# Key norms by float32r products on channels, and a block inversion moved to GpSimd, in a hybrid RWKV-7 / FoX block

## The chip, the cores and the metric

The kernel runs on one core of a Trainium2 chip. The metric is the device time of one execution in microseconds, the median of several runs. The core's engines work from queues of their own: TensorE (products and transposes; PE in the profile, its weight loads PEld), VectorE (DVE), ScalarE (ACT), GpSimd (POOL) and SyncE (SP), which issues most of the DMAs. An instruction waits on semaphores for what it reads and for the buffers that it overwrites, and whatever is behind it in the same queue waits too.

## The reference, cut to what matters

One decoder layer for 256 tokens behind 16 meta tokens (272 rows), width 2048, all in float32. It is an input projection, RWKV-7 time mixing and FoX forgetting attention side by side (16 heads of 64 each), gates, and a SwiGLU network:

```python
def _rms(x, g):
    xf = x * lax.rsqrt(jnp.mean(x * x, axis=-1, keepdims=True) + RMS_EPS)
    return xf * g

def _rwkv7(z, ...):                       # z: r, k, v and three low-rank parts
    ...
    kk = heads(k * k_k)
    kk = kk / jnp.maximum(jnp.sqrt(jnp.sum(kk * kk, axis=-1, keepdims=True)), 1e-12)
    ...
    y = _wkv7_scan(rh, dh, kh, vh, -kk, kk * ah)
    ...                                   # group norm, bonus, gate

def _fox(z, q_g, k_g, f_bias):
    ...
    q = _rms(q.reshape(B, L, FOX_HEADS, HEAD_DIM), q_g)
    k = _rms(k.reshape(B, L, FOX_HEADS, HEAD_DIM), k_g)
    ...                                   # causal softmax with forgetting, times v

def _layer(h, ...):
    proj = _rms(h, n1) @ w_in
    y_a, y_b = _rwkv7(...), _fox(...)
    merged = g_a * (y_a @ w_a) + g_b * (y_b @ w_b)
    h = h + merged @ w_o
    gate, up = jnp.split(_rms(h, n2) @ w_gu, 2, axis=-1)
    return h + (silu(gate) * up) @ w_dn
```

Two places matter here. The keys of both branches are normalised head by head, over 64 channels. And the scan over time is computed in chunks of 64 tokens, for which a unit triangular matrix of each chunk and head has to be inverted.

## The kernel before, in words

**Weights.** All large products read weights in tiles of 128 x 1024 float32. `wload` loads a tile on SP's queue into `raw` (3 buffers, line 318), ScalarE copies it to float32r as `wh` (3 buffers, line 322), and VectorE subtracts to get the remainder `wl` (line 323). A product is then three float32r products (`mm3`, lines 333 to 335), or two with high and low activations side by side (`mm2`, lines 391 to 394).

**Channels on partitions.** In the mixing part the activations lie with 128 channels (two heads of 64) on the partitions and up to 272 tokens along the free axis. A group g (0 to 3) has four heads: two halves m of 128 channels. `rwkv_jobs(g)` makes k, v, r and the low-rank products of a group, `fox_jobs(g)` its q, k and v. In program order: the low-rank part of all heads (`lora_jobs`), then for each group rwkv, fox and two gate jobs (`gate_jobs`, seen as zg), then the remaining gate jobs, the branch products (br), w_o, gate/up and down.

**The written order.** TensorE's order is written out by hand. Each main job calls `slot(ns)` after a few products, which moves a model clock `clock[0]` by the main products' time alone. Everything else of a group runs in generators ("streams", `rwkv_bg`, `fox_bg`, norms) that are advanced by one stage whenever they are due by that clock: a `yield 2900` means "not before 2900 ns of main products from now". So the yields say how far behind a stage the next is placed in TensorE's queue; if its inputs are late, TensorE waits. `pe_mm` and `pe_tr` are the products and transposes of streams (lines 355 and 359). The order on VectorE, ScalarE, GpSimd and SP is chosen by a planner when the kernel is built (except in the first stage); the hardware then keeps it.

**The norms before.** The squares of the keys (sq, sqf) are the stationary operand of float32 products with `bsum` (128 x 2, a column of ones for each head), one for each 128 tokens and half: `head_sums`, seen as ss (rwkv) and fss (fox). That puts the sums with tokens on the partitions, a [128, 12] table. `rsqrt_steps` finds the inverse roots there by an integer start value and two correcting steps on VectorE (lines 259 to 268). `spread` copies each root over 64 columns (ScalarE, line 603) and transposes back (TensorE, kx and fx), and VectorE multiplies the keys (k, kn) by it (lines 696 and 1008). The queries' sums go the same way up to their roots, which later scale the scores (hs, hr).

**The inversion before.** `rwkv_bg` makes the chunk matrices (mat products, NK), sends their diagonal 32 x 32 blocks through DRAM (d1) to a tile `ln` with one block on each of 112 partitions (lines 765 to 773, SP), and runs 31 elimination steps of two small VectorE operations each (lines 834 and 836), a `yield STEP` after each four. Then the result `lx` goes back through DRAM (d2, d3; lines 841 and 843) into `X` (lines 847 and 848), all on SP's queue, where the weight loads of `wload` are too. A `yield LANE` of 24000 separates this from the first product that reads X.

**After that** come four steps of the scan, the group norm, the transposes yT and the output ya; the tile yas is split from it for the branch products (line 459). In `fox_bg` GpSimd makes the bias tables (lines 1067 to 1070) from a broadcast load on SP (line 1064), TensorE the scores (sc), ScalarE the exponentials, and TensorE the outputs (po). GpSimd otherwise does the subtraction of the token shift (`lerp`, line 445), copies and memsets.

Of the kernel before, what the change touches and what calls it, by code (L numbers as in the profile page):

```python
# [9 lines left out]
F32 = mybir.dt.float32  # L10
F32R = mybir.dt.float32r
# [7 lines left out]
P = 128  # L19
# [45 lines left out]
LERP = 2800  # L65
BIAS = 7000
STEP = 1000
NORM = 4200
SUMS = 2000
X_RS = 1400  # L70
X_SPREAD = 1400
X_V = 1900
X_SC = 1600
X_EXP = 1100
X_DIV = 2600
X_PT = 1400
Y_SQ = 1400
Y_SPREAD = 3300
Y_KK = 2900
Y_DECAY = 1400  # L80
Y_AB = 4400
Y_MAT = 2900
Y_NEXT = 2300
Y_BONUS = 1200
# [13 lines left out]
def hybrid_block(ctx, tc, A, out, dbg=None):  # L98
# [106 lines left out]
    def zt_(name):  # L205
        return rw.tile([P, 274], F32, tag="z", name=name, bufs=ZB)
# [68 lines left out]
    def rstd1():  # L275
        parts = [et(f"{n}1").bitcast(F32R) for n in ("xqh", "xql")]
        split(*parts, xsum)

        def back():
            ps = aux_ps("rms1")[:, :L]  # L280
            for i in range(4):
                nc.tensor.matmul(ps, allones, parts[i % 2][:, i // 2, :], start=i == 0, stop=i == 3)
            ms = zt_("ms1")[:, :L]
            nc.vector.tensor_scalar(ms, ps, 1.0 / D, RMS_EPS, op0=ALU.mult, op1=ALU.add)
            rt = zt_("rt1")[:, :L]
            rsqrt_small(None, rsb, ms, rt, None)
        return back
# [65 lines left out]
    def pe_mm(out_, lhsT, rhs, start, stop, skip=False):  # L353
        clock[2] += 4 * max(lhsT.shape[-1], rhs.free_size()) / 2.4
        nc.tensor.matmul(out_, lhsT, rhs, start=start, stop=stop, skip_group_check=skip)
# [223 lines left out]
        nc.vector.tensor_scalar(eps1, rs1, RMS_EPS, None, op0=ALU.mult)  # L579
        gate_done.append(1)  # L580

    def tiles(n):
        return [(n - T, P), (n - P, P)] + ([(0, NMETA)] if n > T else [])

    def head_sums(dst, sqs, n, name):


        ps = aux_ps(name)  # L590
        if n > T:
            nc.gpsimd.memset(dst, 1.0)
        for i, (t0, w) in enumerate(tiles(n)):
            for m in range(2):
                c = 4 * i + 2 * m
                pe_mm(ps[:w, c:c + 2], sqs[m][:, t0:t0 + w], bsum, start=True, stop=True)
        return [(dst[:w, 4 * i:4 * i + 4], ps[:w, 4 * i:4 * i + 4]) for i, (_, w) in enumerate(tiles(n))]

    def spread(rs, m, n, name):

        tl = tiles(n)
        ex = et(name).rearrange("p m t -> p (m t)")[:, :3 * P].rearrange("p (i c) -> p i c", c=P)
        nc.scalar.activation(ex[:, :len(tl), :].rearrange("p i (h d) -> p i h d", h=2),
                             rs.rearrange("p (i m h) -> p i m h", m=2, h=2)[:, :, m, :].unsqueeze(3).to_broadcast(
                                 [P, len(tl), 2, HD]), AF.Copy)

        def back():
            ps = aux_ps(name)[:, :n]
            for i, (t0, w) in enumerate(tl):
                pe_tr(ps[:, t0:t0 + w], ex[:w, i, :], ident[:w, :w])  # L610
            return ps
        return back


    def rwkv_jobs(g):
# [54 lines left out]
    def rwkv_bg(g, box):  # L670
# [26 lines left out]
        yield Y_KK  # L697

        cs = et(f"cs{g}")
# [131 lines left out]
        for s_ in range(31):  # L831
            n, w = s_ // 3 + 1, 31 - s_
            tv, xv = lt[:, 0:n, s_ + 1:], lx[:, 0:n, s_ + 1:]
            nc.vector.tensor_tensor(tv, lx[:, 0:n, s_:s_ + 1].to_broadcast([LANES, n, w]),
                                ln[:, s_:s_ + 1, s_ + 1:].to_broadcast([LANES, n, w]), op=ALU.mult)
# [143 lines left out]
    def fox_jobs(g):  # L979
# [3 lines left out]
        vv = fx.tile([P, 2, L], F32, tag="vv", name=f"vv{g}", bufs=1)  # L983
        jobs = []
        ready = []
        hs = fx.tile([P, 20], F32, tag="hs", name=f"hs{g}", bufs=4)
        hr = fx.tile([P, 20], F32, tag="hs", name=f"hr{g}", bufs=4)
        done = []

        def sums(sqs, dst, n):  # L990
            c = slice(0, 8) if dst is qn else slice(8, 20)
            for i, (d, ps) in enumerate(head_sums(hs[:, c], sqs, n, f"fss{g}{n}")):
                nc.vector.tensor_scalar(d, ps, 1.0 / HD, eps1[:d.shape[0], i:i + 1], op0=ALU.mult, op1=ALU.add)
            done.append(1)
            return
            yield

        def norms():
            while len(done) < 2:
                yield  # L1000
            yield from rsqrt_steps(fx, hr, hs, [P, 20], "ht")
            yield X_RS

            nc.vector.tensor_tensor(hs[:, 0:8], hs[:, 0:8], hr[:, 0:8], op=ALU.mult)
            backs = [spread(hr[:, 8:20], m, L, f"fx{g}{m}") for m in range(2)]
            yield X_SPREAD
            for m in range(2):
                nc.vector.tensor_tensor(kn[:, m, :], kn[:, m, :], backs[m](), op=ALU.mult)
            yield
            ready.append(1)  # L1010

        def post(dst, n):
            def f(pss):
                sqs = []
                for m in range(2):
                    ps = pss[m]
                    if dst is vv:
                        nc.scalar.activation(dst[:, m, :], ps[:, :n], AF.Copy)
                        continue
                    sq = fx.tile([P, L], F32, tag="sqf", name=f"sqf{g}", bufs=3)  # L1020
                    if dst is qn:
                        halves(dst[:, m, :], ps)
                        nc.scalar.activation(sq[:, :n], dst[:, m, :], AF.Square)
                    else:
                        nc.scalar.activation(sq[:, :n], ps[:, :n], AF.Square)
# [13 lines left out]
    def fox_bg(g, qn, kn, vv, hs, hr, ready):  # L1039
# [351 lines left out]
```

## Time and profile before

| | before |
|---|---|
| median of 3 runs | 1566.58 us (1565.39 to 1569.84) |
| profiled execution, its own time | 1564.75 us |
| its span in the profile | 1563.0 us |
| granted TensorE clock | 1.0 throughout |
| TensorE busy | 1553.5 us |
| VectorE busy | 1015.7 us |
| ScalarE busy | 766.8 us |
| GpSimd busy | 104.3 us |
| HBM read / written | 274.43 MB / 7.19 MB |

The groups of the mixing part fill roughly the first 610 us, the gate and branch products follow, and the network fills the rest from about 824 us. In the profile's rows a start is in us from the span's start, then the duration in us, the engine, the line, the operation, what is written and read, and a count; a bracket gives the idle time of the engine just before and what ended it. SPq is SP issuing DMAs. Products overlap on TensorE, so that the sum of their durations is more than the time they take: intervals between starts tell their price.

### The profile page before, as it was taken

To read this page: it belongs to the slowest core of one execution; us is meant where nothing else is said; L and a number is where in the kernel's file an instruction comes from. 1 tells how busy PE (TensorE), PEld (TensorE's weight loads), DVE (VectorE), ACT (ScalarE), POOL (GpSimd) and SP (SyncE) were. 2 spreads that over 40 slices of the span, in tenths; PEclk is the share of its full clock that TensorE was granted. 3 is DMA by queue.
4 is the path that set the end of the run, shared out by engine and by line. 5 is a ranking of instruction groups with operands and counts; after the bars stand their busy time and mean duration, and the time that the engine had idled before them with its cause. 6 is when DMAs were issued, how large, how long until landed. Compare 5 with 4: busy or idle time off the path is not lost.

```text
span 1563.0 us, 26173 instructions
## 1 busy us (share of the span) xinstructions
PE 1553.5 (99%) x10225; PEld 1366.3 (87%) x10225; DVE 1015.7 (65%) x1854; ACT 766.8 (49%) x1118; POOL 104.3 (7%) x194
## 2 busy tenths in 40 slices
PE   9999999999999999999999999999999999999998
PEld 9999988989889888999888888888888888888887
DVE  7878688677768856875655666566566656444443
ACT  6655455465445544654445554454445544333332
POOL 2121103102203100000000000000000000000000
PEclk9999999999999999999999999999999999999999
DMA  7556546546545566777666666666666666666664
GB/s 243 173 154 173 158 126 179 157 119 168 166 135 148 161 182 192 248 225 227 189 182 179 188 186 190 188 188 189 188 189 189 185 193 187 188 202 199 187 200 131
DMA packets 211483, 283.33 MB, mean 181 GB/s; under 512 B 23888, under 2 KB 128352, under 8 KB 211360
## 3 DMA queue, kind: packets, MB, share of 16 engines
q1 hardware_dynamic: 206752, 277.53, 60.8%
q10 hardware_dynamic: 4608, 4.13, 0.8%
q8 instruction: 80, 1.31, 0.4%
q14 instruction: 43, 0.35, 0.1%
HBM read 274.43 MB, written 7.19 MB: 180 GB/s over the span
## 4 chain that ended last, share of the span: by engine, by line
PE 94%; DVE 3%; DMA 1%; ACT 1%; issue 1%; SPq 0%; POOL 0%; DVEq 0%; ACTq 0%
PE up L392 10%; PE gt L392 10%; PE zg L392 7%; PE dn L1255 5%; PE dn L1253 5%; PE dn L1254 5%; PE up L394 5%; PE gt L394 5%; PE zg L394 3%; PE f L333 2%; PE f L392 2%; PE f L335 2%; PE f L334 2%; PE br L334 2%; PE br L335 2%; PE br L333 2%
## 5 line engine op out<-in xcount | busy, mean ns | idle before, releaser
L323 DVE TENSOR_TENSOR wl<-raw,wh 128x1024 fp32r<-128x1024 f32 (+1 forms) x496 | 605.3, 1221 | 439.7 <-ACT wh L322 437.8
L322 ACT ACTIVATE wh<-raw 128x1024 fp32r<-128x1024 f32 (+1 forms) x496 | 521.2, 1052 | 624.5 <-PE dn L1254 144.4
L392 PE MATMUL gt<-hts,wh 128*128 128x512 f32 x704 | 245.0, 394 | 0.0
L392 PE MATMUL up<-hts,wh 128*128 128x512 f32 x704 | 244.9, 394 | 0.0
L394 PE MATMUL gt<-hts,wl 128*128 128x256 f32 x660 | 186.2, 282 | 0.0
L394 PE MATMUL up<-hts,wl 128*128 128x256 f32 x660 | 186.0, 282 | 0.0
L392 PE MATMUL zg<-xhl,wh 128*128 128x512 f32 x512 | 184.3, 403 | 0.0
L392 PEld LDWEIGHTS up<-hts,wh 128*128 128x128 f32 x704 | 130.1, 188 | 26.4
L392 PEld LDWEIGHTS gt<-hts,wh 128*128 128x128 f32 x704 | 130.1, 188 | 26.3
L1254 PE MATMUL dn<-wh,acl 128*128 128x512 f32 x352 | 139.5, 396 | 0.0
L1253 PE MATMUL dn<-wh,ach 128*128 128x512 f32 x352 | 139.5, 396 | 0.0
L1255 PE MATMUL dn<-wl,ach 128*128 128x512 f32 x352 | 139.5, 396 | 0.0
L394 PE MATMUL zg<-xhl,wl 128*128 128x256 f32 x480 | 135.0, 281 | 0.0
L394 PEld LDWEIGHTS up<-hts,wl 128*128 128x128 f32 x660 | 124.7, 189 | 1.8
L394 PEld LDWEIGHTS gt<-hts,wl 128*128 128x128 f32 x660 | 124.7, 189 | 1.8
L392 PEld LDWEIGHTS zg<-xhl,wh 128*128 128x128 f32 x512 | 94.5, 188 | 20.8 <-issue 1.8
L394 PEld LDWEIGHTS zg<-xhl,wl 128*128 128x128 f32 x480 | 90.6, 189 | 1.1
L1255 PEld LDWEIGHTS dn<-wl,ach 128*128 128x128 f32 x352 | 66.3, 188 | 16.2
L1254 PEld LDWEIGHTS dn<-wh,acl 128*128 128x128 f32 x352 | 66.3, 188 | 16.2
L1253 PEld LDWEIGHTS dn<-wh,ach 128*128 128x128 f32 x352 | 66.3, 188 | 16.1
L333 PE MATMUL f<-xhl,wh 128*128 128x272 f32 x256 | 77.7, 303 | 0.0
L335 PE MATMUL f<-xhl,wl 128*128 128x272 f32 x256 | 73.8, 288 | 0.0
(459 smaller groups left out, 2777.6 us busy)
## 6 DMA issues: line engine op xcount, KB each, us to landing
raw<-in_w_gate_up_dram SPq DMA_DIRECT2D x176, 512.0 KB, 3.6
raw<-in_w_in_dram SPq DMA_DIRECT2D x160, 512.0 KB, 4.2
raw<-in_w_down_dram SPq DMA_DIRECT2D x88, 512.0 KB, 4.7
raw<-in_w_o_dram SPq DMA_DIRECT2D x32, 512.0 KB, 4.6
raw<-in_w_branch_a_dram SPq DMA_DIRECT2D x16, 512.0 KB, 3.9
raw<-in_w_branch_b_dram SPq DMA_DIRECT2D x16, 512.0 KB, 3.8
zgd<-zg ACTq DMA_DIRECT2D x30, 128.0 KB, 2.4
gate<-zgd SPq DMA_DIRECT2D x15, 256.0 KB, 5.8
```

The lines of the kernel that those rows point to most:

```text
L322: nc.scalar.activation(wh[:prow, cs_], raw[:prow, cs_], AF.Copy)
L323: nc.vector.tensor_tensor(wl[:prow, cs_], raw[:prow, cs_], wh[:prow, cs_].bitcast(F32), op=ALU.subtract)
L333: nc.tensor.matmul(ps, wh, ah, start=first, stop=False)
L334: nc.tensor.matmul(ps, wh, al, start=False, stop=False)
L335: nc.tensor.matmul(ps, wl, ah, start=False, stop=last)
L392: nc.tensor.matmul(ps.rearrange("p (a t) -> p a t", a=2), wh, act, start=first, stop=last)
L394: nc.tensor.matmul(ps[:, :T], wl, act[:, 0, :], start=False, stop=False)
L1253: nc.tensor.matmul(box[t], ah[:, kt, ts_], wh[:, k, :], start=first, stop=False)
L1254: nc.tensor.matmul(box[t], al[:, kt, ts_], wh[:, k, :], start=False, stop=False)
L1255: nc.tensor.matmul(box[t], ah[:, kt, ts_], wl[:, k, :], start=False, stop=last)
```

## The change

- The norms of the keys stay on channels. The squares are split into a high and a low float32r half, and two products with `bones` (128 x 128, a block of ones for each head) give every channel the sum of its head, for all 272 tokens at once. VectorE adds the floor, ScalarE finds a first inverse root as Exp(-0.5 Ln x) and squares it, and GpSimd makes one correcting step (3/2 - x y y / 2) and multiplies the keys. `spread` and the third token tile of `head_sums` go; the queries keep their table, now of 8 columns. For FoX the floor is a table `epsw` over the tokens, made once in the first stage.
- The two operations of each elimination step go from VectorE to GpSimd.
- Waits between stages (the yields) get new values.

```diff
-NORM = 4200
-SUMS = 2000
-X_RS = 1400
-X_SPREAD = 1400
+NORM = 6500
+SUMS = 3500
...
-Y_SPREAD = 3300
-Y_KK = 2900
+N_SUM = 2000
+N_ROOT = 3600
+Y_KK = 5500
 Y_DECAY = 1400
-Y_AB = 4400
+Y_AB = 5000
...
+    epsw = xp.tile([P, L], F32, tag="epsw", name="epsw")
...
             nc.vector.tensor_scalar(ms, ps, 1.0 / D, RMS_EPS, op0=ALU.mult, op1=ALU.add)
+            nc.vector.tensor_scalar(epsw, ms, RMS_EPS, None, op0=ALU.mult)
...
+    def head_norms(xs, root, dst, floor, name):
+        parts = []
+        for m in range(2):
+            hi, lo_ = (zt_(f"{n}{name}{m}")[:, :L].bitcast(F32R) for n in ("nh", "nl"))
+            split(hi, lo_, xs[m])
+            parts.append((hi, lo_))
+        yield N_SUM
+        pss = []
+        for m in range(2):
+            ps = aux_ps(f"{name}{m}")[:, :L]
+            for i, part in enumerate(parts[m]):
+                clock[2] += L / 2.4
+                nc.tensor.matmul(ps, bones, part, start=i == 0, stop=i == 1)
+            pss.append(ps)
+        for m in range(2):
+            floor(xs[m], pss[m])
+        ys = root()
+        zs = [zt_(f"nz{name}{m}")[:, :L] for m in range(2)]
+        for m in range(2):
+            nc.scalar.activation(ys[m], xs[m], AF.Ln)
+        for m in range(2):
+            nc.scalar.activation(ys[m], ys[m], AF.Exp, scale=-0.5)
+        for m in range(2):
+            nc.scalar.activation(zs[m], ys[m], AF.Square)
+        yield N_ROOT
+        for m in range(2):
+            nc.gpsimd.tensor_tensor(xs[m], xs[m], zs[m], op=ALU.mult)
+            nc.gpsimd.tensor_scalar(xs[m], xs[m], -0.5, 1.5, op0=ALU.mult, op1=ALU.add)
+            nc.gpsimd.tensor_tensor(ys[m], ys[m], dst[:, m, :], op=ALU.mult)
+            nc.gpsimd.tensor_tensor(dst[:, m, :], ys[m], xs[m], op=ALU.mult)
...
         yield Y_SQ
-        kn_ = rw.tile([P, 12], F32, tag="kn", name=f"kn{g}", bufs=2)
-        kr_ = rw.tile([P, 12], F32, tag="kn", name=f"kr{g}", bufs=2)
-        for d, ps in head_sums(kn_, [sq[:, m, :] for m in range(2)], L, f"ss{g}"):
-            nc.vector.tensor_scalar(d, ps, 1e-24, None, op0=ALU.max)
-        yield from rsqrt_steps(rw, kr_, kn_, [P, 12], "kt")
-        backs = [spread(kr_, m, L, f"kx{g}{m}") for m in range(2)]
-        yield Y_SPREAD
-        for m in range(2):
-            nc.vector.tensor_tensor(kk[:, m, :], kk[:, m, :], backs[m](), op=ALU.mult)
+        def root():
+            y = et(f"ny{g}")
+            return [y[:, m, :] for m in range(2)]
+        yield from head_norms([sq[:, m, :] for m in range(2)], root, kk,
+                              lambda x_, ps: nc.vector.tensor_scalar(x_, ps, 1e-24, None, op0=ALU.max), f"ss{g}")
         yield Y_KK
...
-            nc.vector.tensor_tensor(tv, lx[:, 0:n, s_:s_ + 1].to_broadcast([LANES, n, w]),
-                                ln[:, s_:s_ + 1, s_ + 1:].to_broadcast([LANES, n, w]), op=ALU.mult)
-            nc.vector.tensor_tensor(xv, xv, tv, op=ALU.add)
+            nc.gpsimd.tensor_tensor(tv, lx[:, 0:n, s_:s_ + 1].to_broadcast([LANES, n, w]),
+                                    ln[:, s_:s_ + 1, s_ + 1:].to_broadcast([LANES, n, w]), op=ALU.mult)
+            nc.gpsimd.tensor_tensor(xv, xv, tv, op=ALU.add)
...
+        def k_norms(sqs):
+            def root():
+                y = fx.tile([P, 2, L], F32, tag="bias", name=f"fy{g}", bufs=1)
+                return [y[:, m, :] for m in range(2)]
+            yield from head_norms(sqs, root, kn,
+                                  lambda x_, ps: nc.vector.scalar_tensor_tensor(
+                                      x_, ps, 1.0 / HD, epsw, op0=ALU.mult, op1=ALU.add), f"fk{g}")
             ready.append(1)
...
-                    spawn(sums(sqs, dst, n), SUMS)
-                    if dst is kn:
-                        spawn(norms(), PREP)
+                    spawn((q_norms if dst is qn else k_norms)(sqs), SUMS)
...
-        while not ready or not gate_done:
+        while len(ready) < 2 or not gate_done:
             yield X_V
```

More of the change, by code (lines that the diff above doesn't have):

```diff
@@ L580, in forget_gate, with head_sums @@
         gate_done.append(1)
-    def tiles(n):
-        return [(n - T, P), (n - P, P)] + ([(0, NMETA)] if n > T else [])
-    def head_sums(dst, sqs, n, name):
+    def head_sums(dst, sqs, name):
         ps = aux_ps(name)
-        if n > T:
-            nc.gpsimd.memset(dst, 1.0)
-        for i, (t0, w) in enumerate(tiles(n)):
+        for i in range(2):
             for m in range(2):
                 c = 4 * i + 2 * m
-                pe_mm(ps[:w, c:c + 2], sqs[m][:, t0:t0 + w], bsum, start=True, stop=True)
-        return [(dst[:w, 4 * i:4 * i + 4], ps[:w, 4 * i:4 * i + 4]) for i, (_, w) in enumerate(tiles(n))]
@@ L599, in spread @@
[L599 to L612, printed above, removed]
+                pe_mm(ps[:, c:c + 2], sqs[m][:, i * P:(i + 1) * P], bsum, start=True, stop=True)
@@ new lines, in head_sums @@
+        return [(dst[:, 4 * i:4 * i + 4], ps[:, 4 * i:4 * i + 4]) for i in range(2)]
+    def head_norms(xs, root, dst, floor, name):
[28 more added lines that the diff above has]
+            nc.gpsimd.tensor_tensor(dst[:, m, :], ys[m], xs[m], op=ALU.mult)
@@ L985, in fox_jobs, with sqf, q_norms @@
         ready = []
[L986 to L1009, printed above, removed]
+        hs = fx.tile([P, 8], F32, tag="hs", name=f"hs{g}", bufs=4)
+        hr = fx.tile([P, 8], F32, tag="hs", name=f"hr{g}", bufs=4)
+        def sqf(m):
+            return fx.tile([P, L], F32, tag="sqf", name=f"sqf{g}{m}", bufs=3)
+        def q_norms(sqs):
+            for i, (d, ps) in enumerate(head_sums(hs, sqs, f"fss{g}")):
+                nc.vector.tensor_scalar(d, ps, 1.0 / HD, eps1[:, i:i + 1], op0=ALU.mult, op1=ALU.add)
+            yield from rsqrt_steps(fx, hr, hs, [P, 8], "ht")
+            nc.vector.tensor_tensor(hs, hs, hr, op=ALU.mult)
+            ready.append(1)
+        def k_norms(sqs):
[5 more added lines that the diff above has]
+                                      x_, ps, 1.0 / HD, epsw, op0=ALU.mult, op1=ALU.add), f"fk{g}")
             ready.append(1)
@@ L1019, in f @@
                         continue
-                    sq = fx.tile([P, L], F32, tag="sqf", name=f"sqf{g}", bufs=3)
+                    sq = sqf(m)
                     if dst is qn:
@@ L1024, in f @@
                     else:
-                        nc.scalar.activation(sq[:, :n], ps[:, :n], AF.Square)
+                        nc.scalar.activation(sq, ps[:, :n], AF.Square)
                         nc.scalar.activation(dst[:, m, :], ps[:, :n], AF.Copy, scale=qk8)
```

## The prediction

> **What bounds the kernel now.** I read the page first (busy shares, then the chain that ended last), then TensorE's own waits, then the order of instructions around each block that the change touches.
>
> ```profile
> span 1563.0 us, 26173 instructions
> PE 1553.5 (99%) x10225; PEld 1366.3 (87%) x10225; DVE 1015.7 (65%) x1854; ACT 766.8 (49%) x1118; POOL 104.3 (7%) x194
> PE 94%; DVE 3%; DMA 1%; ACT 1%; issue 1%; SPq 0%; POOL 0%; DVEq 0%; ACTq 0%
> PE f L392 <- ACT sig L655: 0.7, 1, 0.7
> ```
>
> TensorE is busy for 99% and is 94% of the chain; its waits are single ones such as the 0.7 us shown. A product taken off TensorE therefore shortens the run, as long as nobody else becomes late; freeing VectorE (65%) by itself gives nothing, since TensorE hardly ever waits for it. So I price TensorE's work, and then look for new lateness.
>
> **TensorE's part.** These are TensorE's rows around the four blocks that go, group 0:
>
> ```profile
> 77.59 1.15 PE L355 MATMUL ss<-bsum,sq 128*128 128x2 f32 x12
> ...
> 79.01 0.28 PE L394 MATMUL f<-xhl,wl 128*128 128x256 f32 x1
> 79.12 0.39 PE L392 MATMUL f<-xhl,wh 128*128 128x512 f32 x1
> 79.35 0.28 PE L394 MATMUL f<-xhl,wl 128*128 128x256 f32 x1
> ...
> 85.38 0.29 PE L335 MATMUL f<-xhl,wl 128*128 128x272 f32 x1
> 85.51 1.07 PE L359 MATMUL kx<-ident,kx 128*128 128x128 f32 x6
> ...
> 86.74 0.29 PE L334 MATMUL f<-xhl,wh 128*128 128x272 f32 x1
> ...
> 101.98 1.13 PE L355 MATMUL fss<-bsum,sqf 128*128 128x2 f32 x12
> ...
> 103.27 0.29 PE L334 MATMUL f<-xhl,wh 128*128 128x272 f32 x1
> ```
>
> Busy times overlap here, so a block's price is read from starts. The ss block delays the product that follows the next one from 77.59 + 0.23 (the step from 79.12 to 79.35) to 79.01: 1.19 us. kx: 86.74 - 85.51 - 0.13 = 1.10. The keys' fss block: 103.27 - 101.98 - 0.13 = 1.16. fx is six transposes of the same shapes as kx: 1.10. Together 4.55 us for each of the four groups, 18.2 us. The queries' fss block stays. What comes in is two norms x 2 halves x 2 float32r products of 128x272 with the block of ones; products of that shape start 0.13 us apart (85.38, 85.51), so 8 x 0.13 = 1.0 us a group, 4.0 us. Net: 14.2 us less. It has no other end: both kinds stand in these rows.
>
> **The inversion on GpSimd.** 62 small two-input operations a group leave VectorE and go to GpSimd. What they cost there no row shows; the nearest:
>
> ```profile
> L834 DVE TENSOR_TENSOR lt<-lx,ln 112x84 f32<-112x84 f32 (+23 forms) x124 | 30.3, 244 | 2.5
> 2.27 0.89 POOL L138 TENSOR_SCALAR_AFFINE_SELECT mup<-mup 64x64 f32<-64x64 f32 x4
> ...
> 398.39 0.73 POOL L1069 TENSOR_TENSOR b<-b,cmask 128x256 f32<-128x256 f32 x1
> 399.08 0.74 POOL L1070 TENSOR_TENSOR bias<-bias,cmask 128x256 f32<-128x256 f32 x1
> 399.76 0.10 POOL L436 MEMSET z<- 128x1 f32 x1
> ...
> 145.73 1.88 POOL L1070 TENSOR_TENSOR bias<-bias,cmask 128x256 f32<-128x256 f32 x1
> 145.79 1.21 DVE L323 TENSOR_TENSOR wl<-raw,wh 128x1024 fp32r<-128x1024 f32 x1
> L1069 POOL TENSOR_TENSOR b<-b,cmask 128x256 f32<-128x256 f32 x8 | 7.8, 974 | 0.0
> 123.80:153.40 29.60, 29.60 (x202) 26.50 (x201) 26.70 (x93) 14.88 (x26) 5.82 (x7) 1.00 0.62 175
> 123.80:153.40 29.60, 7.59 (x31) 1.00 0.62 175
> ```
>
> A group's inversion handles 64 elements per operation in the mean (the sum of n*w over 31 steps is 1991). With one input, 64 elements take 0.22 us (0.89 for four). Two inputs take 0.69 us for 256 (398.39 to 399.08), of which 0.10 is what a memset of one element takes: 0.10 + 64 x 0.59/256 = 0.25, and since each operation reads what the one before wrote I add 0.05: 0.30 us, 18.6 us for 62. That is solo. Beside VectorE it stretches: the L1070 that met a 1.21 us wl took 1.88 in place of 0.74; the mean of the eight L1069 is 0.974, 1.41 times the step of 0.69. So 26 us, with ends 13.6 us (0.22 each, undisturbed) and 50 us (2.7 times, as the 1.88).
>
> The Trainium skill, "SBUF — State Buffer", section "Who interferes with whom", says that a VectorE instruction with two SBUF inputs and a GpSimd one that reads SBUF block each other for a whole instruction; the 1.88 agrees. By that rule, with VectorE's other work holding (26.70 - 2 x 7.59)/29.6 = 39% of the window (the last two rows: all of VectorE, and L834 alone; L836 has the same count and shapes), the inversion would take an estimated 18.6/0.61 = 30 us rather than 26; what that does to the sum stands with the second rival.
>
> Who waits for it: the copies out (d from lx), the loads of X and all weight loads behind them, on SP's one queue.
>
> ```profile
> L773 SPq DMA_DIRECT2D ln<-d x16: 250/295/307, 114.1 to 496.5; - x16
> 139.60 12.23 SPq L318 DMA_DIRECT2D raw<-in_w_in_dram  x4
> 153.37 1.98 SPq L841 DMA_DIRECT2D d<-lx  x3
> 161.06 1.52 SPq L318 DMA_DIRECT2D raw<-in_w_in_dram  x3
> ...
> 391.87 13.19 SPq L318 DMA_DIRECT2D raw<-in_w_in_dram  x5
> ...
> 415.48 1.52 SPq L318 DMA_DIRECT2D raw<-in_w_in_dram  x3
> 421.71 1.05 PE L355 MATMUL po<-pT,vt 128*64 128x256 f32 x6 [1.66 <-ACT pT L1110]
> ```
>
> In group 0 the last ln loads are issued at some 115 and land about 4 us later, at 119; SP reaches the copies at 153.4. That is 34 us: 26 fit, 50 do not. In that time GpSimd also has 5.8 us of bias and lerp work (the window's POOL column), so 26 becomes about 32. The inversion moves to later together with what waits for it, since the waits written out for it (STEP, LANE) are unchanged. Cost: nothing in the likeliest case. If the cover is gone, SP's gap between weight loads shows the price: 151.8 to 161.1 = 9.2 us passes without a wait in group 0; in group 2, 405.1 to 415.5 = 10.4 us, and TensorE then idles 1.66 us because ScalarE stands at a late weight tile with pT behind it. So about 1 us is spare, and from there each us costs one. The same lateness has a second road: a lerp's subtraction (L445) stands behind the inversion's steps on GpSimd, VectorE's L448 behind that, and wl behind L448. It is the same microseconds, so I do not add it again.
>
> **The norms' chain.** Per norm ScalarE now does two copies (split), two Ln, two Exp, two Square, against two kx/fx copies; VectorE two subtractions and two floors against the small steps of the root; GpSimd eight operations of 272 elements, 0.10 + 272 x 0.59/256 = 0.73 each, 5.8 us solo, 8.2 stretched by 1.41. Engine time is there (ACT 49%, POOL 7%). On the path stands the next product that reads the result, mat.
>
> ```profile
> L554 ACT ACT_TABLE_LOAD x1 | 1.3, 1283 | 0.0
> L555 ACT ACT_TABLE_LOAD x1 | 1.3, 1283 | 0.0
> 70.13 1.28 ACT L655 ACT_TABLE_LOAD   x1
> 71.42 0.86 ACT L655 ACTIVATE sig<-sig,vcol 128x272 f32<-128x272 f32 x2
> ...
> L720 DVE TENSOR_TENSOR bk<-k,cs 128x512 f32<-128x512 f32 x4 | 2.7, 684 | 0.0
> ...
> 97.84 1.09 PE mat L355 x16
> 115.88 0.91 PE fx L359 x6
> 134.34 0.91 PE sc L355 x8
> ```
>
> L554 (Exp) and the L555 (Ln) behind it each loaded a table, so I count two loads: 2 x 1.28 + 6 x 0.43 = 5.1 us of ScalarE. Chain from the product: two floors and four scalings on VectorE, by the 0.68 of the like bk step about 4.3; ScalarE 5.1; GpSimd 8.2: 17.6 us. The yields between them give 3.6 + 5.5 + 1.4 + 5.0 = 15.5 us of main products; the last 8.7 of the old chain (2.9 + 1.4 + 4.4) lasted 97.8 - 85.5 = 12.3 us on the chip, because side products and other streams lie between, so 15.5 become about 21. It is covered, with some 3 us over. In fox the scores come 18 us after fx (115.9 to 134.3), which covers GpSimd too. The new bias slot use (fy) makes SP's bias load wait for GpSimd's last step; that is 2.4 us late (8.2 against 5.8), under the spare of an ordinary gap: nothing. The norm takes all six buffers of the z ring (two nh, nl and nz each); lerps and gate evictions that need one wait until the products, or GpSimd, are done with them. At that point of a group only gate evictions come, two in some 11 us, so I cost it at nothing; without that cover it is the 8.2 us of GpSimd in front of an eviction, part of the first rival. The one added step for epsw is a 272-element operation of VectorE in the first stage, under 0.5 us, beside TensorE's loras. VectorE's own 15 us a group that go, and the memsets that go from GpSimd, free nothing that TensorE waits for.
>
> A burst of 5.1 us on ScalarE also holds back weight tiles (wh). The nearest row is the 0.7 us wait behind L655, a load of 1.28 and four sigmoids, 3.0 us. Two bursts a group, one of which I let cost 0.7: 4 x 0.7 = 3 us; ends 0 (each lies in a gap) and 8 x (0.7 + 5.1 - 3.0) = 22.
>
> **The tail.** A rwkv stream becomes longer by 2.9 (norms) + 0.6 (Y_AB) + 2.3 (NORM) = 5.8 us of main products.
>
> ```profile
> 607.00 0.60 PE L359 MATMUL yT<-ident,Y 128*128 128x128 f32 x4
> 624.99 0.61 ACT L459 ACTIVATE yas<-ya 128x512 fp32r<-128x512 f32 x1
> ```
>
> By the same ratio, 12.3 for 8.7, that is 8 us on the chip: the last group's yT goes from 607 to about 615, ten before the splits of ya at 625, with gate products beside it: nothing; without the cover at most the 8 us.
>
> **Sum.** 1564.75 (the profiled execution: span 1563.0 and 1.75 around it) - 18.2 + 4.0 + 3 = 1553.6. The median of the runs is 1.8 above that execution, so 1555.
>
> **Rivals.** First, the norms are late: if GpSimd's eight operations take twice their solo time (11.6) and the 15.5 us of yields last only 18, mat waits 21.0 - 18 = 3 us a group, 12 us: 1567, no change. The ratio of 1.41 just used speaks against it; for it speaks that GpSimd's rows stretch more where VectorE is fullest (1.88 for 0.74). The Trainium skill, "ScalarE: Activation LUTs", section "Table sets: the hidden batching unit", says that Ln followed by Exp needs one load, since one set has both; L554 and L555 ran the other way round and cannot show it. By that rule the burst would be an estimated 3.8 us, and the time 1553.
>
> Second, on the other side: SP stands at the copies for GpSimd. SP's order is fixed when the kernel is built; if it puts the copies where an undisturbed inversion ends (18.6 us) while the chip takes 26, SP and all weight loads stand 7.4 us, of which 1 is spare: 6.4 x 4 = 26 us, 1555 + 26 = 1581. It outweighs the gain from about 4.5 us of lateness a group. For it: GpSimd's two-input work stretches, and the gap is at its limit already. Against: 34 us of room where the copies lie now, and VectorE, 15 us lighter there, stretches less. By the blocking rule cited above the lateness would be an estimated 11.9 us, and the time near 1599.
>
> Third, the products removed were hidden anyway, weights setting the pace: 1566. Against it: in the window of the inversion TensorE is busy for all of 29.6 us, DMA for 0.62, and VectorE's 90% becomes 39%.
>
> **How the numbers follow.** Forecast 0.57 (1549 to 1561); norms late or nothing gained 0.17 (1562 to 1571); SP held 0.26 (1572 to 1600). A measurement tells about 0.3%, 5 us, from no change. Faster 0.57, same 0.17, slower 0.26. The range leaves out the upper half of the last case and little below the first: 1549 to 1584.
>
> **What would show it.** Right: ss, kx and fx gone, eight bones products a group at 0.13 us steps, L834's successor on POOL with 25 to 32 us from first to last, SP's gap around the copies at 9 to 10 us, TensorE's waits under 8 us in all. Wrong: SP waiting for POOL at the copies, weight tiles late in the four windows, mat waiting for POOL or DVE.

## The result, and the profile after

The changed kernel takes 1662.21 us (median, 1660.28 to 1664.72) against 1565.99 us before on the same chip: 1.0611 times, with a 95% interval of 1.0586 to 1.0637. It is 96 us slower, where 11 us less were forecast. All that was lost lies in the mixing part: behind it, from 700 to 1100 us, TensorE is busy for 399.86 of 400 us, as before.

The page of the changed kernel: span, busy time, TensorE in 40 slices, its granted clock, the chain that ended last.

```profile
span 1663.0 us, 26048 instructions
PE 1560.7 (94%) x10113; PEld 1369.6 (82%) x10113; DVE 967.6 (58%) x1563; ACT 802.8 (48%) x1184; POOL 242.3 (15%) x498
PE   9997799599959977999999999999999999999999
PEclk9998799799979998999999999999999999999999
PE 73%; POOL 9%; DVE 4%; ACT 3%; DMA 2%; issue 2%; SPq 1%; POOLq 0%; ACTq 0%; DVEq 0%
```

TensorE was 94% of the chain and is 73%; GpSimd, which had none, has 9%. There are four holes in TensorE's row, one for each group, and beside each the clock dips, which was 1.0 throughout before. The waits of the engines name the holes (what was waited for; us in total, times, longest):

```profile
PE k L334 <- ACT wh L323: 53.5, 3, 18.3
PE zg L393 <- ACT wh L323: 22.4, 4, 18.2
...
SPq L849 <- POOL b L1070: 65.1, 3, 22.2
SPq L849 <- POOL z L437: 21.0, 1, 21.0
...
DVE XT L921 <- DMA X<-d: 79.1, 4, 21.2
```

Four times TensorE stops 17 to 18 us (71.7 in all, the 18.2 of zg among them; the other waits on wh are short) for a weight tile (wh), SP stands 21 to 22 us at the copies out of lx (L849) for GpSimd, and VectorE stands as long at the transposes of X. The instruction named behind POOL is the next one on that queue; what SP needs is the last L844 ahead of it, as the rows of group 1 show:

```profile
282.92 11.32 SPq L319 DMA_DIRECT2D raw<-in_w_in_dram  x6
295.52 0.34 SPq L1067 DMA_DIRECT2D bias<-ncd  x1
317.70 1.93 SPq L849 DMA_DIRECT2D d<-lx  x3
...
325.33 6.84 SPq L319 DMA_DIRECT2D raw<-in_w_in_dram  x4
...
287.69 0.24 POOL L842 TENSOR_TENSOR lt<-lx,ln 112x31 f32<-112x31 f32 x1
...
303.87 1.23 POOL L844 TENSOR_TENSOR lx<-lx,lt 112x85 f32<-112x85 f32 x1
...
312.16 0.30 POOL L842 TENSOR_TENSOR lt<-lx,ln 112x64 f32<-112x64 f32 x1
312.54 0.32 POOL L844 TENSOR_TENSOR lx<-lx,lt 112x64 f32<-112x64 f32 x1
...
317.44 0.23 POOL L844 TENSOR_TENSOR lx<-lx,lt 112x11 f32<-112x11 f32 x1
...
303.49 1.38 DVE L324 TENSOR_TENSOR wl<-raw,wh 128x1024 fp32r<-128x1024 f32 x1 [0.52 <-ACT wh L323]
326.03 0.45 DVE L921 STREAM_TRANSPOSE XT<-X 128x256 f32<-128x256 f32 x1 [21.16 <-DMA X<-d]
...
330.57 0.60 PE L334 MATMUL k<-xhl,wh 128*128 128x272 f32 x1 [18.33 <-ACT wh L323]
...
332.46 0.43 PE L335 MATMUL k<-xhl,wh 128*128 128x272 f32 x1
332.68 0.43 PE L336 MATMUL k<-xhl,wl 128*128 128x272 f32 x1
```

The inversion lasts from 287.7 to 317.7, 30.0 us. SP is through with its loads and the bias load at 295.9 and stands until 317.7; the next weight load is issued at 325.3, 31 us after the last one, where the gap before was 9 to 10. The planner had moved the copies: with the inversion on VectorE (the first experiment) SP has four or five weight loads between the bias load and the copies, here none (in group 0 the copies stand ahead of the bias load as well). Last, after the hole products of this shape start 0.22 us apart (332.46, 332.68), not 0.13. The windows of the same stretch (PE busy is the first time behind the length; the clock is the third number from the end):

```profile
300.00:305.00 5.00, 5.00 (x44) 4.52 (x43) 2.64 (x4) 2.48 (x6) 4.37 (x9) 1.00 0.09 30
...
315.00:320.00 5.00, 0.00 (x0) 0.00 (x0) 0.00 (x0) 0.00 (x0) 4.37 (x14) 0.50 0.11 18
...
330.00:335.00 5.00, 3.99 (x17) 3.67 (x18) 2.94 (x4) 2.64 (x3) 0.00 (x0) 0.53 0.70 206
```

So the time can be split in three. Idle is span less busy. "At low clock" sums, over windows of 5 us, TensorE's busy time by (1 - clock). "Work" is busy less that.

| kernel | span | idle | at low clock | work |
|---|---|---|---|---|
| before | 1563.0 | 9.5 | 0.0 | 1553.5 |
| changed | 1663.0 | 102.3 | 16.7 | 1544.0 |
| norms alone | 1583.2 | 30.7 | 8.6 | 1543.9 |
| norms alone, no table loads | 1565.7 | 22.5 | 0.0 | 1543.2 |

The products did get shorter, by 9.5 us; waits cost 92.8 and the lower clock behind them 16.7: 100.0 us of span.

### The profile page after: what moved, and what is told of

It reads as the page before. It is cut to its first block, busy times and chain, and to the rows that moved or that the text cites. A ratio compares the mean times of both kernels' runs of the same rounds, so it can differ in the third digit from the quotient of the medians.

```text
span 1663.0 us, 26048 instructions
## 1 busy us (share of the span) xinstructions
PE 1560.7 (94%) x10113; PEld 1369.6 (82%) x10113; DVE 967.6 (58%) x1563; ACT 802.8 (48%) x1184; POOL 242.3 (15%) x498
## 4 chain that ended last, share of the span: by engine, by line
PE 73%; POOL 9%; DVE 4%; ACT 3%; DMA 2%; issue 2%; SPq 1%; POOLq 0%; ACTq 0%; DVEq 0%
PE up L393 10%; PE gt L393 10%; PE dn L1258 5%; PE dn L1257 5%; PE dn L1256 5%; PE up L395 5%; PE gt L395 5%; PE zg L393 3%; POOL lx L844 3%; POOL lt L842 3%; PE br L335 2%; PE br L336 2%; PE br L334 2%; PE wo L1257 2%; PE wo L1256 2%
## 5 line engine op out<-in xcount | busy, mean ns | idle before, releaser
L393 PE MATMUL zg<-xhl,wh 128*128 128x512 f32 x512 | 190.7, 413 | 22.4 <-ACT wh L323 22.4
L334 PE MATMUL k<-xhl,wh 128*128 128x272 f32 x128 | 40.6, 317 | 53.5 <-ACT wh L323 53.5
```

The source lines that it names most:

```text
L334: nc.tensor.matmul(ps, wh, ah, start=first, stop=False)
L393: nc.tensor.matmul(ps.rearrange("p (a t) -> p a t", a=2), wh, act, start=first, stop=last)
```

## Experiments

**Norms alone.** Both operations of the inversion back on VectorE.

```diff
-            nc.gpsimd.tensor_tensor(tv, lx[...], ln[...], op=ALU.mult)
-            nc.gpsimd.tensor_tensor(xv, xv, tv, op=ALU.add)
+            nc.vector.tensor_tensor(tv, lx[...], ln[...], op=ALU.mult)
+            nc.vector.tensor_tensor(xv, xv, tv, op=ALU.add)
```

> The changed kernel with the inversion's two operations back on VectorE; the norms stay as changed, and SP has its copies where they were before. Theory (the 96 us come from SP standing at the copies for GpSimd, and from nothing else): no stall of 18 us per group is left, TensorE has 14 us less to do than before, and the time is 1549 to 1560, some 0.6% under before. Rival (the norms' own work on ScalarE and GpSimd is late as well, or takes back what the products give): 1566 or more, with waits of TensorE on mat, on k or on weight tiles behind ScalarE's Ln and Exp.

Measured: 1584.46, 1.0123 times before (1.0109 to 1.0137). The holes of 18 us are gone, but the rival holds: the norms lose 19 us by themselves. First SP's copies and VectorE's first and last inversion steps in group 1, to set beside the rows of the changed kernel:

```profile
280.75 14.56 SPq L319 DMA_DIRECT2D raw<-in_w_in_dram  x5
296.37 1.92 SPq L849 DMA_DIRECT2D d<-lx  x3
...
269.19 0.18 DVE L842 TENSOR_TENSOR lt<-lx,ln 112x31 f32<-112x31 f32 x1
...
296.16 0.18 DVE L844 TENSOR_TENSOR lx<-lx,lt 112x11 f32<-112x11 f32 x1
```

VectorE takes 27.2 us from the first step to the last, since its other work lies between the steps; in the kernel before it took 29 to 32 us in the four groups, and GpSimd takes 30 to 31. So the inversion became hardly longer. Counted from the issue of the last ln load, lx is ready after 38 to 40 us in the kernel before, 31 to 34 us here and 35 us in the changed kernel. So lx came 1 to 4 us later than here, and sooner than in the kernel before, while SP stood 21 to 22 us: its copies had been placed four or five loads earlier.

Waits of this kernel, and ScalarE's rows around the longest wait for R:

```profile
PE u L356 <- ACT R L874: 5.1, 4, 2.4
PE zg L395 <- DVE wl L324: 4.4, 3, 2.0
PE pv L360 <- ACT ya L967: 4.0, 3, 2.8
...
SPq L1067 <- POOL kn L624: 20.4, 2, 10.4
...
DVE lt L842 <- DMA ln<-d: 7.3, 1, 7.3
...
L614 ACT ACT_TABLE_LOAD x11 | 14.1, 1283 | 0.2
L616 ACT ACT_TABLE_LOAD x11 | 14.1, 1283 | 0.2
...
209.80 1.28 ACT L614 ACT_TABLE_LOAD   x1
...
211.86 1.28 ACT L616 ACT_TABLE_LOAD   x1
...
213.81 0.73 ACT L618 ACTIVATE nzss<-ny 128x272 f32<-128x272 f32 x2
214.45 0.25 ACT L874 ACTIVATE R<-rhs 128x128 f32<-128x128 f32 x1
...
130.00:135.00 5.00, 2.11 (x6) 1.60 (x7) 4.73 (x15) 3.45 (x4) 0.04 (x1) 0.71 0.82 238
135.00:140.00 5.00, 5.00 (x22) 4.13 (x22) 3.37 (x10) 1.06 (x1) 0.00 (x0) 0.61 0.96 294
```

Two sources can be read: ScalarE's burst of 4.7 us (209.8 to 214.5) with the scan's R behind it, and SP at the bias load (L1067), which waits for GpSimd's last norm step since fy lies in the bias buffer; the ln loads are behind it. The waits themselves are short, but after two of 2.8 and 1.3 us at 131 the clock is down: 0.71 and 0.61 in the means of these two windows, and 0.50 to 0.55 in windows of 1 us from 132 to 139.

**Inversion alone.** The kernel before with the same two operations on GpSimd.

> The kernel before with only the inversion's two operations moved to GpSimd; the norms stay as before. Theory (SP's stand is the inversion's alone): per group SP waits some 20 us for GpSimd and TensorE some 18 us for weights, as in the changed kernel, and the 10 to 14 us that the products give are missing, so 1662 + 12 = about 1674 (1655 to 1690). Rival (the norms' operations on GpSimd, some 6 us a group, and ScalarE's bursts are part of the lateness): 1600 to 1645, with less than 15 us of SP's wait per group.

Measured: 1630.20, 1.0414 (1.0400 to 1.0428). SP stood four times 17 to 18 us at the copies (35.3 + 33.8 us in all): neither the 20 and more of the theory nor the under 15 of the rival. TensorE's longest stops were shorter, 11.0 and 11.7 us behind the softmax (pT) and 4.8 to 6.6 us for weight tiles. 65 us for the inversion alone and 19 for the norms alone make 84 of the 96; the other 12 are the two together.

**Copies from GpSimd's queue.** Norms and inversion as changed; the 13 transfers from lx to X and X0 go from `nc.sync` to `nc.gpsimd`.

> The changed kernel, with the copies out of lx and the loads of X and X0 issued from GpSimd's queue, not SP's; the inversion is still GpSimd's and takes its 30 us. Theory (what costs is that weight loads stand behind the copies): SP no longer waits for GpSimd, TensorE's waits for weights go under 10 us in all, and the time is 1550 to 1562. Rival (the inversion itself is too slow for those who need X, whoever issues the copies): TensorE's or the evictions' waits on X's users stay, 1590 to 1650.

Measured: 1643.37, 1.0503 (1.0488 to 1.0517); 19 us better than the changed kernel, and the rival holds:

```profile
PE k L336 <- DVE wl L324: 41.2, 3, 14.8
...
DVE XT L921 <- DMA X<-d: 78.7, 4, 21.0
```

SP no longer stands at the copies. But VectorE's order had been made for the same early X: it stands 21 us at the transposes, with a weight tile's subtraction (wl) behind them. Taking away the first stop showed the second, almost as long.

**Copies where they were.** The copies stay on SP, but come into the program 20 us of main products later, tied to the last weight load issued by then.

```diff
+        yield 20000
+        with tc.issue_after(last_raw[0].ins):
             for j in range(3):
                 nc.sync.dma_start(d2[...], lx[...])
             ...
-        yield LANE
+        yield LANE - 20000
```

> The changed kernel, with the copies still on SP but emitted 20 us of main products after the inversion's last step, which puts them behind the same number of weight loads as in the kernel before (five more per group than in the changed kernel); the products that use X come when they did. Theory (the planner's place of the copies makes the loss): in groups 1 to 3 there are 27 us from the ln loads to the copies, in group 0 34, and the inversion needs 5 + 30, so SP waits 0 to 8 us a group in place of 22; 1555 + 3 x 7 = about 1576 (1555 to 1595). Rival (the place does not matter, GpSimd's slowness is felt at X's users): over 1630.

Measured: 1611.89, 1.0299 (1.0285 to 1.0313). 50 of the 77.8 us that the inversion costs beside the changed norms (1662.2 less 1584.5) are back, so the place in the queues is the larger part, but 27 stay, six more than the theory had: the time lies between the two forecasts. VectorE doesn't wait at the transposes any more; what waits now:

```profile
SPq L854 <- POOL b L1075: 35.3, 4, 9.6
...
PE ppt L363 <- DVE s L1106: 21.9, 4, 7.9
...
DVE k L452 <- POOL z L440: 28.4, 3, 10.0
```

SP still stands up to 9.6 us at the copies, but TensorE's waits for weight tiles are short again (at most 3.9 us). VectorE stands at the lerps' last step for GpSimd, and the softmax (s) is late for ppt; ppt's 21.9 us are nearly all of the 22.8 us that TensorE idles longer than with the norms alone (53.5 against 30.7). GpSimd's own queue is the third that was ordered for a short inversion.

**Bias and lerps off GpSimd**, on top of the last: their subtractions and the four bias operations on VectorE.

> The kernel with the copies where they were (norms and inversion as changed, copies on SP behind five more weight loads), with the bias tables and the lerps' subtractions on VectorE and no longer on GpSimd, where they stood behind the inversion's steps. Without this TensorE waits 21.9 us on ppt (behind the softmax's s, behind the bias tables), and the time is 1611.9, 27 above that of the norms alone. Theory (that third queue, GpSimd's own, holds the rest of the inversion's loss): 1611.9 - 22 - 6 for the clock = 1584 (1580 to 1592). Rival (the rest is VectorE slowed by GpSimd beside it, or X late): 1605 or more.

Measured: 1609.27 (1600.98 to 1613.40), 1.0273 (1.0243 to 1.0303): nothing gained, the rival's number. Of its two causes, VectorE slowed by GpSimd isn't seen in the weight tiles: a wl takes 1225 ns in the mean here, 1221 in the kernel before; for X VectorE waits 4.9 us in all. ppt waits 4.8 us, not 21.9, but VectorE now stands 17.7 us at the bias tables for SP's load, which waits for copies of GpSimd (L787, L791: 28.0, of which 20.9 were there with the norms alone), and TensorE 12.5 us for NK. **Lerps alone off GpSimd** (with their one-column memset):

> The changed kernel with the copies behind five more weight loads (1611.9), and with the lerps' subtraction and their one-column memset on VectorE; the bias tables stay on GpSimd. With the copies moved alone, VectorE stood 28.4 us in three waits at a lerp's last step (k), for a subtraction that lay behind the inversion and a bias table on GpSimd, and the softmax behind it on VectorE was late for ppt (21.9 us of TensorE). Theory (what is left of the inversion's loss there is this third queue): VectorE's waits on k go, ppt waits 8 us or less in all, 1611.9 - 14 - 4 = 1594 (1586 to 1600). Rival (the bias tables behind the inversion hold the softmax as long anyway): 1605 or more, ppt's wait unchanged.

Measured: 1607.13, 1.0274 (1.0258 to 1.0289). The rival holds:

```profile
PE ppt L363 <- DVE s L1106: 18.9, 4, 5.8
...
DVE s L1095 <- POOL b L1077: 22.8, 4, 6.5
```

VectorE's wait has moved from the lerp to the softmax, for the bias table behind the inversion. So both kinds of GpSimd's work wait there; no run brought the 27 us back, and that they are GpSimd's queue is read from the waits, not shown by a cure.

**Inversion spread out.** The written waits raised.

```diff
-                yield STEP          # 1000
+                yield ISTEP         # 3600
...
-LANE = 24000
+LANE = 6000
```

> The changed kernel (norms and inversion as changed, copies on SP), with the written waits between the inversion's steps raised from 1000 to 3600 ns of main products after each eight operations, which is what eight take on GpSimd (8 x 0.43 to 0.48 us), and the wait behind them cut from 24000 to 6000, so that X is used when it was. The planner then places the copies, the transposes of X and GpSimd's other work by the time that the chip needs, not by a shorter one. Theory (the inversion's loss comes from orders planned for a short inversion): SP's and VectorE's waits of 20 us are gone, and the time is that of the norms alone, 1584, plus little: 1580 to 1595. Rival (30 us of GpSimd's one queue do not fit whatever the order): 1605 or more.

Measured: 1640.58, 1.0479 (1.0461 to 1.0496). The rival's number, but this doesn't decide: the first copy still stood as early (SP waited up to 24.3 us for the last L845, 86.8 in all as against 86.1), since the written waits order TensorE's side and GpSimd went through its steps without idling (30 to 33 us); only the later copies came to lie between loads, and TensorE's four holes were 10 to 12 us.

**Half the inversion.** `eng = nc.vector if s_ < 16 else nc.gpsimd`.

> The changed kernel with the first 16 of 31 elimination steps on VectorE again and 15 (30 operations) on GpSimd. GpSimd's part is then 30 x 0.45 = 13.5 us. In the changed kernel SP's copies stand three (group 0: five) loads earlier than with the inversion on VectorE; here two to three loads earlier. Theory (loss in proportion to GpSimd's operations): the 77.8 us between the changed kernel (1662.2) and the norms alone (1584.5) become half: 1623 (1610 to 1635). Rival (only lateness beyond a spare of some us costs, so the shorter part is nearly free): under 1600.

Measured: 1639.43, 1.0478 (1.0462 to 1.0494), beyond both: 30 of 62 operations cost 55 of the 77.8 us. The half on VectorE has to share that engine, and lx is not done sooner: in group 1 VectorE's steps last from 280.4 to 294.9 and GpSimd's from 300.1 to 314.3, 40 us after the last ln load was issued (35 in the changed kernel). SP stood there 14 us (60.4 in the four groups, against 86.1), with no weight load between 300.0 and 322.2. So this run does not halve SP's stand. Its copies stand two loads earlier than with the inversion on VectorE; in the changed kernel it is five (group 0: four), not three (group 0: five) as was expected.

**The norms: fy off the bias buffer.**

```diff
-                y = fx.tile([P, 2, L], F32, tag="bias", name=f"fy{g}", bufs=1)
+                y = et(f"fy{g}")
```

> The norms alone (inversion on VectorE), with FoX's root fy in the ring of [128, 2, 272] tiles (tag e) and no longer in the one bias buffer, so that SP's bias load need not wait for GpSimd's last norm step. With the norms alone SP stood twice 10 us at that load (20.4 us in two waits), the ln loads behind it were late, VectorE stood 7.3 us at the inversion's first step in group 0, and TensorE stopped 4.1 us at 131 and 2.0 us at 532, each with some 2 us of lower clock behind it. Theory (that shared buffer is a third to a half of the norms' loss): 1584.5 - 4.1 - 2.0 - 4 = 1574 (1570 to 1578), and SP's two long waits are gone. Rival (the scores' tables are late by GpSimd's chain itself, whatever the buffer): 1582 or more.

Measured: 1578.85, 1.0090 (1.0076 to 1.0103): SP's waits for kn are gone, 5.6 us better where 10 were expected.

**The norms: no table loads.**

```diff
-            nc.scalar.activation(ys[m], xs[m], AF.Ln)
+            nc.scalar.activation(ys[m], xs[m], AF.Exp, scale=-1e-6)
...
-            nc.scalar.activation(ys[m], ys[m], AF.Exp, scale=-0.5)
+            nc.scalar.activation(ys[m], ys[m], AF.Exp, scale=-9.0)
```

> The norms alone, with Ln replaced by a second Exp, so that ScalarE needn't change its table between the two (the roots are then constants and the output is not the reference's; the operations are as many and as large). Of 22 table loads in the eight norms most should go, about 1.28 us each. Theory (ScalarE's burst of 4.7 us, with the scan's R behind it, is a part of the norms' loss): the waits of TensorE on R (5.1 us in four) go, with 2 us of clock, 1584.5 - 7 = 1577 (1573 to 1580). Rival (the loads lie beside other work): 1583 to 1586.

Measured: 1569.92, 1.0037 (1.0024 to 1.0049). 14.5 us better, twice what was expected, for 18 loads less (the four that are left are as many as the kernel before had at the decay's Exp, L706):

```profile
PE u L356 <- ACT R L874: 1.8, 2, 1.0
...
L614 ACT ACT_TABLE_LOAD x4 | 5.1, 1283 | 0.1
```

In the profiled executions idle falls by 8.2 us, to 22.5, and the time at low clock by 8.6, to nothing: there half of the gain is the clock. This one is the fastest of the five executions; the granted clock of the others is 0.996 to 0.998, so in them some waits still lower it. **Both edits**:

> The norms alone with both edits: Ln replaced by a second Exp (constant roots, the output is not the reference's) and fy in the ring of [128, 2, 272] tiles. Theory (14.6 and 5.6 us are separate losses of the norms): 1584.5 - 20.2 = 1564 (1561 to 1567), TensorE idle 16 to 18 us, so that the 10 us of products saved are eaten by what is still late. Rival (both work through the same lateness, the end of the norm chain, and do not add): 1568 to 1571.

Measured: 1567.01 (11 runs), 1.0014 (1.0005 to 1.0022). Together they give 17.5 of the 20.1 us; with intervals of some 2 us on each run, whether they add in full can't be told. With 21.1 us idle against 9.5 before, the shorter products are still paid back in many waits of up to 2.4 us.

**The norms: correcting step on VectorE** (the four `nc.gpsimd` lines of `head_norms` to `nc.vector`).

> The norms alone, with their correcting step (eight operations of 272 elements per norm) on VectorE, not GpSimd. VectorE takes some 0.43 us for each in place of GpSimd's 0.76 to 1.1, the chain gets 3 to 5 us shorter, and no weight subtraction (wl) meets a norm step on GpSimd and stretches from 1.2 to 1.7 us. Theory (GpSimd's chain is what makes bias, mat's inputs and ya late): 1565 to 1575, TensorE's waits on ya (4.0) and at 131 (4.1) gone. Rival (VectorE, 28 us longer in all, makes weight tiles late): 1585 to 1595.

Measured: 1583.21, 1.0115 (1.0101 to 1.0129): no change, against both. VectorE stands 24.8 us in all for ScalarE's roots (L621), which is what GpSimd did for it.

**A version from the findings**: the inversion on VectorE, fy off the bias buffer, the first root by the integer start on VectorE.

```diff
-            nc.scalar.activation(ys[m], xs[m], AF.Ln)
...
-            nc.scalar.activation(ys[m], ys[m], AF.Exp, scale=-0.5)
...
+            nc.vector.tensor_scalar(ys[m].bitcast(I32), xs[m].bitcast(I32), -0.5, 1595932665.0, op0=ALU.mult, op1=ALU.add)
+            nc.vector.tensor_tensor(zs[m], ys[m], ys[m], op=ALU.mult)
+            nc.vector.scalar_tensor_tensor(zs[m], xs[m], -1.0, zs[m], op0=ALU.mult, op1=ALU.mult)
+            nc.vector.scalar_tensor_tensor(ys[m], zs[m], R2, ys[m], op0=ALU.add, op1=ALU.mult)
...
+            nc.scalar.activation(zs[m], ys[m], AF.Square, scale=R1)
...
+            nc.gpsimd.tensor_scalar(xs[m], xs[m], -0.5 * R1, 1.5 * R1, op0=ALU.mult, op1=ALU.add)
```

R1 and R2 are the constants of `rsqrt_steps`.

> A version from the findings: norms on channels by the products with ones, inversion on VectorE, fy off the bias buffer, and the first root by the integer start and one step on VectorE (four operations of 272 elements for each half, some 0.45 us each, 29 us in all) instead of Ln and Exp; ScalarE keeps the Square, GpSimd the correcting step. Theory (table loads 14.5 us and the shared buffer 5.6 us are additive): 1584.5 - 20 = 1564 (1559 to 1568), the same as before. Rival (VectorE's added work makes weight tiles late): 1572 or more. Rival (the granted clock stays at 1 and the waits go as well): 1555 or less.

Measured: 1593.32, 1.0181 (1.0165 to 1.0197), worse than the norms alone: the first rival.

```profile
PE zg L395 <- DVE wl L324: 8.8, 7, 2.1
PE zg L393 <- ACT wh L323: 7.3, 3, 2.4
```

VectorE's share is 65% of the span, but its 24 us more (busy 1038.8 against 1014.7) fall where TensorE waits for its weight tiles. No version was found that beats the kernel before.

## Why the prediction was wrong

The second rival's mechanism is what happened; it had a chance of 0.26 and a size of 26 us. By steps:

- **Where SP's copies lie.** The step that failed is "The inversion moves to later together with what waits for it, since the waits written out for it (STEP, LANE) are unchanged. Cost: nothing in the likeliest case". The 34 us of room were measured in an order made for VectorE. The inversion hardly moved to later, for on VectorE it had lasted about as long. The order on SP, VectorE and GpSimd is the planner's, and it moved the copies up by four or five weight loads. The lateness was 21 to 22 us a group, not 7.4: the rival assumed that the planner thinks an undisturbed inversion takes 18.6 us; SP reached the copies 8 to 10 us after its start (8.2 in group 1, 287.7 to 295.9). What the planner reckons with stands in no trace; that it placed the copies for a short inversion is read from their place.
- **The price on GpSimd.** 0.30 us for one of 64 elements was too low. With VectorE standing, the two rows at 312 start 0.38 us apart. 62 x 0.38 = 24 us; most of the rest of the 30.0 are six operations such as the one at 303.87, which met a wl and took 1.23. The 0.05 us added for the dependence between operations came from no row. The estimate by the blocking rule of the Trainium skill, "SBUF — State Buffer", "Who interferes with whom", was 30 us; the stretched row agrees with the rule, but the sum does so by chance: VectorE stood for the last 13 of the 30 us, the six stretched operations make only 5 of the 11 us above the 18.6 forecast for GpSimd alone, and the higher price makes the other 6. The 26 forecast was 4 us off; by the prediction's own 34 us of room that alone would have cost little.
- **"The same microseconds".** The lerps and bias tables behind the inversion were left out of the sum as the same lateness. That is right while SP stands, but by the waits they are a stop of their own: with the copies moved back and VectorE's transposes served, 27 us were left. No run cured it. The transposes on VectorE, the second stop, were not named at all.
- **ScalarE's bursts**, taken at 3 us (ends 0 and 22), measured 14.5 for 18 loads. 16 loads were counted; there were 22, since in FoX's norms of groups 1 to 3 the planner ran the halves one after the other, Ln, Exp, Ln, Exp, with a load each (242.47 to 249.75 in group 1, norms alone). The row that I took as nearest, a wait of 0.7 us behind L655, has one load in a place with room; the scan's R, behind which TensorE waited up to 2.4 us, has none.
- **The table rule.** The Trainium skill, "ScalarE: Activation LUTs", "Table sets: the hidden batching unit", says that Ln followed by Exp needs one load. Here it does not hold: L614 and L616 have 11 loads each in eight norms.
- **The bias buffer.** "2.4 us late ...: nothing" was 10 us, twice (20.4 in all); the ln loads stood behind it on SP. It cost 5.6 us.
- **TensorE's term.** -14.2 forecast, 9.5 to 10.3 measured in work. The block prices were right. In all four groups of the kernel before, the next product starts 1.06 to 1.08 us after an ss or keys' fss block and 1.00 after kx or fx, and the one behind that is late by 0.10 to 0.11; four products with bones take 0.50, in seven of the eight norms without table loads. About 4 us came back on other products that took longer from start to start without a recorded wait, zg most (186.1 to 188.0 us in all). Why they did stays open.
- **The tail** and the cover of the norm chain were right (15.5 x 12.3 / 8.7 is 21.9 rather than 21, which only adds to the cover): TensorE has no wait over 1 us between 550 and 660 us in the kernel with the norms alone, and mat waited 1.2 us once.
- **The clock** was missing from the sum. SP's 86.1 us at the copies became 71.7 us of TensorE's holes, so the spare was about 3.6 us a group, not 1; but "from there each us costs one" leaves out the 16.7 us that came on top.

## What to carry to other kernels

Room measured in an old order is not room in a new one: if a planner places the waiting instructions, ask what it believes of the moved work, and look for each queue that has a consumer or a neighbour of it (here SP and VectorE, each a stop of some 20 us a group, and by its waits GpSimd itself, some 6). Price a burst on an engine by the instruction that stands behind it with no room, and count the table loads that the profile of a like sequence shows. Where TensorE is at 99%, work taken from it is only worth something if less comes late than was taken: here about 10 us of products went, and with both edits to the norms TensorE still idled 11.6 us more than before.

## What the runs showed of the hardware that was not expected

- Waits lower the clock, and the length of a single one doesn't decide. In the kernel before, 1.66 us left it at 1.0. With the norms alone, 2.42 us left it at 1.0, and 2.78 us were followed by a lower one:

```profile
214.76 0.45 PE L356 MATMUL u<-R,X 64*64 64x64 f32 x8 [2.42 <-ACT R L874]
...
388.71 0.69 PE L360 MATMUL pv<-ident,vv 128*128 128x128 f32 x2 [2.78 <-ACT ya L967]
```

Behind the second the clock is 0.50 for some 3 us, behind the waits of 2.8 and 1.3 us at 131 for some 7, and two waits of 0.5 and 1.2 us close together (255.6 and 257.9) do it too. In the long holes it is 0.50 as well, and just after them products of 272 columns start 0.22 us apart, not 0.13. The Trainium skill, "TensorE: Matmul & The Clock Gate", "HAM oscillation — how this bites in real kernels", warns of idle gaps over about 3.4 us; here shorter ones did it. What separates 2.42 from 2.78 us, or from 0.5 and 1.2, no run here shows.
- A small two-input operation on GpSimd whose input is the output of the one before takes, with VectorE idle beside it (changed kernel, group 1, from 312 us on), 0.29 us for 11 elements, 0.33 for 30 and 0.38 for 64 from start to start; most of it does not depend on size.
